# Fifteen 64-byte-row reads behind two input loads in a convolution kernel

## The chip, the cores and the metric

The kernel runs on one core of a Trainium2 chip. The time is device microseconds (us) of one execution. Besides the timed executions one execution was taken by the hardware profiler; the rows that are quoted as profile lines come from that one. Engines are named as in the profile: PE is the matrix engine, PEld its weight load, DVE the vector engine, ACT the scalar engine, POOL the GpSimd engine, SP the SyncE engine, which computes nothing here and issues transfers. A q behind an engine's name is its instruction queue; q0, q1, q10 and so on are queues of transfers, served by 16 DMA engines.

## The reference

The kernel computes a 3x3 convolution with padding 1 of a batch of 16 images, 64 channels in and 128 out, 64 by 64 pixels, in float32 in and out.

```
batch, c_in, h, w, c_out = 16, 64, 64, 64, 128
x_pad = np.pad(x, ((0, 0), (0, 0), (1, 1), (1, 1)), mode='constant')
for b in range(batch):
    for co in range(c_out):
        for ci in range(c_in):
            for kh in range(3):
                for kw in range(3):
                    output[b, co] += weight[co, ci, kh, kw] * x_pad[b, ci, kh:kh+h, kw:kw+w]
```

The input is 16.8 MB, the output 33.6 MB, the weights 0.3 MB.

## The kernel before

Images are taken in pairs: the 64 channels of two images fill the 128 partitions, so there are eight pairs, numbered 0 to 7. Two neighbouring output rows share work: with a row sum `ss` (row 2j plus row 2j+1, line L71) one product with the middle weights serves both. For each pair, four blocks of eight row couples are worked on; in each block PE makes three groups of products (all on line L155): U from `ss`, A and Bt from the 16-bit input `xs`, each for both images into a PSUM tile `acc` (eight of them exist). ACT copies U to `ut` (L169), DVE adds A and `ut` into the even rows of the output tile `ot` (L178) and Bt and `ut` into the odd rows (L181).

Transfers go by three issuing engines. SP issues, in this order, the weights `w_raw` (L42), pair 0 as float32 `x0` (L44), pair 1 as float32 `x1` (L46), and later the stores of the first image of each pair (helper `store`, L111). POOL issues the loads of pairs 2 to 7 straight into 16-bit tiles `xs` (helper `load`, L57): three at the start, three more inside the loop. ACT issues the stores of the second image of each pair, held back until the next block's `ut` copies have been made (also L111). Pairs 0 and 1 are turned to 16 bit on chip by ACT (L96, L175); the row sums of pair 0 are made by DVE, all others by POOL (L71).

`x0`, `x1` and the output tiles share eight 16 KB buffers under the tag `ot`, so stores may run up to four pairs behind the arithmetic. In the last two pairs the stores are cut into halves and quarters.

The order of the work on an engine is that of the program; `keep` fixes it for the copies, sums, loads and held stores. The framework adds all waits. It gives the transfers that SP and ACT issue, in the order of the program, one of eight completion counters in turn; an issue that takes a counter for the second time is preceded by a wait, on the issuing engine, until the counter's previous transfer has landed. Before the change there are 24 such transfers (three loads, 21 stores), so the ninth is the first to wait, and the profile has eight such waits on SP and seven on ACT under L111, of 17 ns each, the first at 52.2 us. POOL's loads have eight counters of their own.

Of the kernel before, what the change touches and what calls it, by code (L numbers as in the profile page):

```python
# [8 lines left out]
F32 = mybir.dt.float32  # L9
# [4 lines left out]
def kernel(  # L14
# [6 lines left out]
    nc = tc.nc  # L21
# [9 lines left out]
    w_flat = weight.rearrange("co ci kh kw -> co (ci kh kw)")  # L31

    const = ctx.enter_context(tc.tile_pool(name="const", bufs=1))
# [10 lines left out]
    nc.sync.dma_start(x0, x_rows[0:128, :, :])  # L44
    x1 = opool.tile([128, H, W], F32, tag="ot", name="x1")
    nc.sync.dma_start(x1, x_rows[128:256, :, :])  # L46
    cuts = [(0, 18), (18, 34), (34, 50), (50, 64)]
    ident = const.tile([128, 128], F16)
    make_identity(nc, ident)
# [168 lines left out]
```

## Time and profile before

| what | value |
|---|---|
| median of three timed executions | 127.23 us (127.17 to 127.58) |
| profiled execution | 128.39 us, of which the span from first to last instruction is 126.6 us |
| PE busy | 106.0 us, from 10.35 us without a longer gap to 115 us |
| DVE, ACT, POOL busy | 83.6, 44.5, 34.6 us |
| HBM read, written | 17.07 MB, 33.55 MB |
| DMA packets | 4330, of them 480 under 512 bytes |
| first load's landing (`x0`) | 9.6 us |
| second load's landing (`x1`) | 19.4 us |
| first store issued by SP, by ACT | 26.23 us, 26.83 us |
| last store issued | 116.48 us |

Busy times are sums over an engine's instructions. The DMA share is the mean busy share of the 16 DMA engines; packets of two queues on one engine may overlap a little, so it can be over 1. A matrix clock of 0.5 at the end of the span belongs to a stretch in which PE has no work.

### The profile page before, as it was taken

Reading aid. Unit: us, or ns where it says so; the run is one execution under the profiler, and the core shown is the slowest. Engines: PE = TensorE matmul, PEld = TensorE weight load, DVE = VectorE, ACT = ScalarE, POOL = GpSimd, SP = SyncE. Lnnn points to the kernel's source line nnn. Section 1 sums busy time; section 2 is a strip of 40 time slices with the busy share of each in tenths; the row PEclk is TensorE's granted clock in tenths of the full one; section 3 lists DMA queues with packets and bytes.
Section 4 is the critical chain, followed back from the end, with each engine's and each line's share of the span. In section 5 each row is a group of like instructions: output and inputs, shape, how many; then the busy total and the mean of one; then the engine's idle time right before and its main releaser. Section 6 shows DMA issues by size and latency. Waiting matters only on the chain.

```text
span 126.6 us, 2412 instructions
## 1 busy us (share of the span) xinstructions
PE 106.0 (84%) x978; PEld 54.3 (43%) x978; DVE 83.6 (66%) x134; ACT 44.5 (35%) x76; POOL 34.6 (27%) x27
## 2 busy tenths in 40 slices
PE   0407999999999999999999999999999999993000
PEld 0303454554555555554555545455554555541000
DVE  0009297787778777877787778777877787777000
ACT  4108937953333333333333333333333333330000
POOL 2700008677007700699770039000000000000000
PEclk9999999999999999999999999999999999999955
DMA  5999999999999999999999999999999999999970
GB/s 148 370 352 331 342 290 210 215 238 318 383 334 331 295 331 357 365 365 344 349 349 362 383 427 419 419 424 450 419 424 419 432 422 414 430 427 418 418 302 22
DMA packets 4330, 44.48 MB, mean 351 GB/s; under 512 B 480, under 2 KB 480, under 8 KB 864
## 3 DMA queue, kind: packets, MB, share of 16 engines
q1 hardware_dynamic: 2016, 21.27, 40.6%
q10 hardware_dynamic: 1440, 16.78, 31.7%
q0 software_dynamic: 864, 6.29, 24.1%
q8 instruction: 7, 0.11, 0.3%
q14 instruction: 3, 0.02, 0.0%
HBM read 17.07 MB, written 33.55 MB: 400 GB/s over the span
## 4 chain that ended last, share of the span: by engine, by line
PE 82%; DMA 7%; DVE 2%; issue 1%; DVEq 0%; SPq 0%
PE acc L155 82%; DMA x<-in_x_dram 7%; DVE ot L178 1%; DVE ss L71 1%; DVE ot L181 0%; DVEq L213 0%; SPq L42 0%; DVEq L178 0%
## 5 line engine op out<-in xcount | busy, mean ns | idle before, releaser
L155 PE MATMUL acc<-xs,Wt 64*128 64x504 f16 (+3 forms) x768 | 88.9, 378 | 0.0
L155 PEld LDWEIGHTS <-Wt 64*128 64x128 f16 x960 | 53.2, 95 | 55.9 <-issue 6.8
L178 DVE TENSOR_TENSOR ot<-acc,ut 128x512 f32<-128x512 f32 x64 | 41.2, 686 | 23.2 <-PE acc L155 18.5
L169 ACT COPY ut<-acc 128x512 f32<-128x512 f32 x64 | 34.4, 589 | 60.8 <-issue 38.5
L181 DVE TENSOR_TENSOR ot<-acc,ut 128x512 f32<-128x512 f32 x64 | 41.1, 685 | 0.0
L155 PE MATMUL acc<-ss,Wt 64*128 64x504 f16 (+1 forms) x192 | 27.0, 384 | 4.6 <-DVE ss L71 4.6
L71 POOL TENSOR_TENSOR ss<-xs 128x1024 f16<-128x1024 f16 x12 | 25.2, 2122 | 10.1 <-DMA xs<-in_x_dram 9.1
L71 DVE TENSOR_TENSOR ss<-x 128x512 f16<-128x512 f32 x4 | 2.6, 686 | 9.6 <-DMA x<-in_x_dram 9.6
L71 POOL TENSOR_TENSOR ss<-x 128x1024 f16<-128x1024 f32 x2 | 4.7, 2356 | 13.4 <-DMA x<-in_x_dram 13.4
L57 POOL DMA_DIRECT2D xs<-in_x_dram x6 | 3.5, 578 | 17.9 <-PE acc L155 16.0
L96 ACT CAST xs<-x 128x1024 f16<-128x1024 f32 (+2 forms) x4 | 4.0, 1053 | 4.0 <-DMA x<-in_x_dram 4.0
L89 PE MATMUL wp<-ident,w 128*64 128x128 f16 x18 | 1.3, 328 | 4.5 <-POOL w L51 4.5
L175 ACT CAST xs<-x 128x1024 f16<-128x1024 f32 x4 | 4.0, 1057 | 0.0
L89 PEld LDWEIGHTS <-w 128*64 128x64 f16 x18 | 1.1, 210 | 4.5 <-POOL w L51 4.5
L91 ACT CAST Wt<-wp 128x384 f16<-128x384 f32 x1 | 0.5, 478 | 3.1 <-PE wp L89 3.1
L91 ACT ACT_TABLE_LOAD x1 | 1.3, 1283 | 0.7 <-PEq L202 0.7
L51 POOL CAST w<-w_raw 128x576 f16<-128x576 f32 x1 | 0.7, 662 | 2.4 <-DMA w_raw<-in_weight_dram 2.4
L98 ACT CAST Wt<-wp 128x384 f16<-128x384 f32 x1 | 0.5, 478 | 0.5 <-DVE Wt L94 0.5
L93 DVE TENSOR_TENSOR Wt<-wp,Wt 128x384 f16<-128x384 f32 x1 | 0.6, 551 | 0.0
L94 DVE TENSOR_TENSOR Wt<-wp,Wt 128x384 f16<-128x384 f32 x1 | 0.5, 548 | 0.0
L99 ACT CAST Wt<-wp 128x384 f16<-128x384 f32 x1 | 0.5, 485 | 0.0
masks.py:199 POOL TENSOR_SCALAR_AFFINE_SELECT ident<-ident 128x128 f16<-128x128 f16 x1 | 0.3, 292 | 0.1
(5 smaller groups left out, 0.6 us busy)
## 6 DMA issues: line engine op xcount, KB each, us to landing
out_dram<-ot SPq DMA_DIRECT2D x6, 2048.0 KB, 19.7
out_dram<-ot ACTq DMA_DIRECT2D x6, 2048.0 KB, 19.3
xs<-in_x_dram POOLq DMA_DIRECT2D x6, 1024.0 KB, 20.5
x<-in_x_dram SPq DMA_DIRECT2D x2, 2048.0 KB, 13.1
out_dram<-ot ACTq DMA_DIRECT2D x4, 1024.0 KB, 11.7
out_dram<-ot SPq DMA_DIRECT2D x3, 1024.0 KB, 12.8
out_dram<-ot SPq DMA_DIRECT2D x2, 512.0 KB, 10.6
w_raw<-in_weight_dram SPq DMA_DIRECT2D x1, 288.0 KB, 3.0
```

The costliest lines, as they stand in the source:

```text
L51: keep(nc.gpsimd.tensor_copy(w16, w_raw))
L57: keep(nc.gpsimd.dma_start(xs[p], x_rows[128 * p : 128 * p + 128, :, :]))
L71: eng.tensor_add(ss[p][:, lo : lo + n, :], v[:, lo : lo + n, 0, :], v[:, lo : lo + n, 1, :])
L89: nc.tensor.matmul(wp[q : q + 64, k * CO : k * CO + CO], w16[:, t::9], ident)
L91: keep(nc.scalar.copy(wrow(G1), wps[1]))
L93: keep(nc.vector.tensor_sub(wrow(G21), wps[2], wrow(G1)))
L96: keep(nc.scalar.copy(xs[0][:, lo:hi, :], x0[:, lo:hi, :]))
L155: nc.tensor.matmul(tiles[b2][:, lo - j0 : hi - j0, c_lo:c_hi], Wt[p0 : p0 + 64, wi, kw, :], rhs, start=i == 0, stop=i == n - 1,)
L169: keep(nc.scalar.copy(ut, U[b2]))
L175: keep(nc.scalar.copy(xs[1][:, lo : lo + 16, :], x1[:, lo : lo + 16, :]))
L178: nc.vector.tensor_add(ots[b2][:, j0 : j0 + RB, 0, :], A[b2], us[b2])
L181: nc.vector.tensor_add(ots[b2][:, j0 : j0 + RB, 1, :], Bt[b2], us[b2])
```

## The change

A spare tile of 16 partitions, 16 rows of 16 float32 each, is made, and behind the load of `x1` fifteen reads are issued from SP. Read n (1 to 15) takes 64 bytes from each of the first n rows of the weights and writes them to the first n partitions of the spare tile. That is 1 + 2 + ... + 15 = 120 rows of 64 bytes, 7,680 bytes together. Nothing reads the spare tile.

```
     nc.sync.dma_start(x0, x_rows[0:128, :, :])
     x1 = opool.tile([128, H, W], F32, tag="ot", name="x1")
     nc.sync.dma_start(x1, x_rows[128:256, :, :])
+    mark = const.tile([16, 16, 16], F32)
+    for n in range(1, 16):
+        nc.sync.dma_start(mark[0:n, n, :], w_flat[0:n, 16 * n : 16 * n + 16])
     cuts = [(0, 18), (18, 34), (34, 50), (50, 64)]
```

The reads take part in the turn of the eight counters: reads 1 to 5 take the five counters not used so far, read 6 that of `w_raw`, read 7 that of `x0`, read 8 that of `x1`, reads 9 to 15 those of reads 1 to 7. The first store (SP) then takes the counter of read 8, the second (ACT) that of read 9. From the ninth store on, each store follows the same earlier store as before.

More of the change, by code (lines that the diff above doesn't have):

```diff
@@ L46 @@
     nc.sync.dma_start(x1, x_rows[128:256, :, :])
+    mark = const.tile([16, 16, 16], F32)
+    for n in range(1, 16):
+        nc.sync.dma_start(mark[0:n, n, :], w_flat[0:n, 16 * n : 16 * n + 16])
     cuts = [(0, 18), (18, 34), (34, 50), (50, 64)]
```

## The prediction

> **What bounds the kernel now.** I began with the chain of waits on the page, which ends on PE:
>
> ```profile
> PE 82%; DMA 7%; DVE 2%; issue 1%; DVEq 0%; SPq 0%
> ```
>
> Read alone, this says that only the landing of x0 at 9.6 us and 104 us of products matter. But the chain stops at the last DVE sum, 116.45 us into a span of 126.6 us; behind it only stores run. So I read the page's slices and then a table of stretches (columns: length, busy time and count of PE, PEld, DVE, ACT, POOL, granted clock, DMA share, GB/s):
>
> ```profile
> DMA  5999999999999999999999999999999999999970
> DMA packets 4330, 44.48 MB, mean 351 GB/s; under 512 B 480, under 2 KB 480, under 8 KB 864
> ```
>
> ```profile
> 4.40:9.60 5.20, 1.31 (x18) 1.23 (x19) 0.00 (x0) 0.48 (x1) 1.70 (x4) 1.00 1.01 381
> 9.60:19.50 9.90, 9.15 (x66) 4.29 (x67) 7.56 (x13) 6.78 (x10) 0.02 (x1) 1.00 1.04 315
> 19.50:26.00 6.50, 6.50 (x64) 3.36 (x62) 5.05 (x9) 5.92 (x8) 4.67 (x2) 1.00 1.01 210
> ...
> 80.00:100.00 20.00, 20.00 (x190) 10.17 (x186) 15.79 (x26) 6.60 (x13) 0.00 (x0) 1.00 1.01 428
> ...
> 117.00:120.00 3.00, 0.00 (x0) 0.00 (x0) 0.00 (x0) 0.00 (x0) 0.00 (x0) 1.00 1.00 414
> 120.00:123.00 3.00, 0.00 (x0) 0.00 (x0) 0.00 (x0) 0.00 (x0) 0.00 (x0) 0.58 0.82 347
> 123.00:126.60 3.60, 0.00 (x0) 0.00 (x0) 0.00 (x0) 0.00 (x0) 0.00 (x0) 0.50 0.07 30
> ```
>
> The share is 1.0 in every stretch from 4.4 to 120 us. The 210 GB/s at 19.5 us is no slack: those are pairs 2 to 4, counted at the 16-bit size written, while twice as much is read. So two bounds lie close together: PE is never idle from 10.35 us on, and the DMA engines have work from 2 to about 122.5 us (0.82 of the 3 us behind 120). The one that ends the kernel is the transfers. At the last issue (116.48 us) about 6 us of work is still queued on every DMA engine, of which the last megabyte itself is 2.5 us at 428 GB/s; arithmetic could end 3.5 us later before the DMA engines ran dry. And the end is that of one DMA engine: the last SP store's sixteen completions, in the trace's landing records, come at 119.4 to 122.6 us for thirteen of them, then 124.2, 124.5 and 125.7.
>
> It follows what to ask of the change: does it give the last DMA engine more work, or does it hold an engine by more than 3.5 us?
>
> **SP's queue.** Start, length, instruction; the loads and the first stores on SP (the third row merges two issues and the time between), then ACT around its first store:
>
> ```profile
> 1.17 0.42 SPq L44 DMA_DIRECT2D x<-in_x_dram  x1
> 1.65 0.42 SPq L46 DMA_DIRECT2D x<-in_x_dram  x1
> 26.23 13.15 SPq L111 DMA_DIRECT2D out_dram<-ot  x2
> ```
>
> ```profile
> 26.16 1.07 ACT L169 COPY ut<-acc 128x512 f32<-128x512 f32 x2 [0.20 <-ACT xs L175]
> 26.83 0.37 ACTq L111 DMA_DIRECT2D out_dram<-ot  x1
> 29.33 1.07 ACT L169 COPY ut<-acc 128x512 f32<-128x512 f32 x2 [2.10 <-DVE ot L181]
> ```
>
> One issue takes 0.42 us and the next follows 0.06 later, so fifteen cost 15 x 0.48 = 7.2 us of SP, which stands idle from 2.07 to 26.23 us. That is cover enough without waits. With the turn of the counters: reads 1 to 5 are out by 4.5 us; read 6 wants w_raw, landed at 3.7, and is out at 5.0; read 7 waits for x0 (9.6) and is out at 10.1; read 8 waits for x1 (19.4) and is out at 19.9; reads 9 to 15 need seven times 0.48, to 23.3 us at the soonest. Behind them on SP stands only the first store, with 2.9 us in hand: cost 0. If that cover went, a store issued later would cost nothing up to the 3.5 us above.
>
> **Waits on landings.** Reads 1 to 7 stand behind x1 in q1 on each DMA engine they use, so x0 and x1 land as before; PE's start, POOL's row sums (19.48) and ACT's casts (20.7) don't move: 0. Even if x1 came later, POOL's sums of pair 1 end at 24.2 us, and PE wants them at 28.4. From 19.4 on the small reads share the engines with pairs 3 and 4 on q0. Between 9.6 and 19.5 us, where x1 and pair 2 ran side by side, the queues had about equal time, row by row; a row of q0 takes 0.63 us (mean of 768 packet records). If a small read waits for one such row, seven are through by 19.4 + 4.4 = 23.8 us, read 8 lands at about 24.5 and read 9 at 25.1: both ahead of the stores that take their counters. If the completion write waits for a row of its own, the seven take 8.8 us; read 8 lands at 29.5 and read 9 at 30.7. Then SP's first store is 3.2 us late and ACT's 3.9 us late; ACT stands still until 31.1 instead of copying at 29.33, 1.8 us late. PE has eight PSUM tiles, four groups, about 3.2 us of lead; nothing is lost there, or at most 1.8 us of the 3.5. The DMA engines are fed meanwhile by pair 4 and by pair 5, issued at 26.02 (2 MB read, 5 us). I take 0, with 0 to 1.8 us of held arithmetic, hidden at the end, as the bounds.
>
> **Work on the DMA engines.** This is what can't hide. The packet records have four sizes: 16,384 bytes in 611 ns, 8,192 (stores) in 309, 4,096 in 159, 2,304 in 93. The last three lie on one line, 9 ns plus 37.5 ns per KB; carried on to 64 bytes it gives 11 ns, an estimate. A completion write of 4 bytes takes 7 to 22 ns, mean 12; every transfer before the change has sixteen (30 transfers, 480 packets under 512 bytes on the page). No row shows a transfer of fewer than 16 rows. Spread evenly, 120 rows are 7.5 on each DMA engine: 7.5 x 11 = 0.08 us, and 15 completions x 12 ns = 0.18 us at most, 0.09 if only engines that carry rows write one. I take the middle of 0.17 and 0.26: 0.2 us. The low end is 0, if the last engine carries none of it; below that, -1.2 us if the last engine's lag over the next (125.7 against 124.5) went away, for which no row speaks. The high end: each row as dear as the nearest row of a load, 93 ns, plus 22 ns, fifteen on one engine: 1.7 us; 0.9 us with 7.5. A first packet of w_raw took up to 714 ns, its latency with nothing ahead of it; later ones of the same ring took 93, and the small reads run beside rows already in flight, so I leave 714 out.
>
> The Trainium skill, in "DMA: Bandwidth & Descriptors", section "Why a DMA increments its semaphore by 16 and not by 1", says that such a transfer uses only as many DMA engines as divide its row counts, the lowest-numbered ones; the first engine would get fifteen rows and the sixteenth none. The same page, "Latency and other measured facts", calls engines 7 and 15 the slow ones as a rule. By the two, the last engine here would get eight rows or none, 8 x 23 ns = 0.2 us or 0, instead of my even spread; no record here names the engine.
>
> The spare tile takes 1 KB in each partition, and no buffer count changes: 0. The end waits for the same counters: 0.
>
> **Sum.** Profiled execution 128.39 (span 126.6 plus 1.8 around it) + 0.2 = 128.6 us. It lies 0.9% above the median of the timed runs, so I carry the difference, not the sum: 127.23 + 0.2 = 127.4 us, no change within 0.3% (0.38 us, about what a measurement of this kernel can tell from none).
>
> **Rivals.** First, slower by dear small packets: place, the last DMA engine between 19.4 and 30 us; price, 0.9 us with 7.5 rows at 115 ns, 128.1 us; 128.9 us with fifteen. It decides as soon as a read costs that engine over 25 ns with fifteen of them, 51 ns with 7.5. For it: the DMA share of 1.0, so nothing is absorbed; against it: the straight line through the packet times and the 12 ns completions. The Trainium skill's "DMA: Bandwidth & Descriptors", "Specifications", speaks for it: under 512 bytes the engine reads, modifies and writes. It gives no price, and no run here shows one for data; by it the time would be this rival's.
>
> Second, slower by a held ACT: read 9 lands so late that ACT's first store holds the copies beyond the 3.5 us in hand. For it: the two-turn reckoning gives 1.8 us of it already; against it: it needs twice that. At 5 us of delay the time is 127.2 + 1.5 + 0.2 = 128.9 us.
>
> Third, faster: the reads or the shifted first stores change which queue an engine serves first, and the last engine's lag of 1.2 us shrinks. 126.0 us if all of it goes, 126.7 with half. For it: the last engine is decided by small things; against it: work is only added.
>
> Fourth, the reads are served in gaps, or not at all: 127.2 us, within the bound.
>
> **How the numbers follow.** Forecast 0.40 and the fourth rival 0.07: same 0.47. Dear packets 0.30, held ACT 0.06, and 0.05 for the forecast's own sum overrun past 0.38 us by a few completions: slower 0.41. Third rival 0.12: faster. The range from 126.8 (half the lag gone and scatter) to 128.6 (dear packets between 7.5 and fifteen rows) leaves about a tenth on each side. The likeliest case's own range is 127.2 to 127.6.
>
> **What would show it.** SP: fifteen more issues of about 0.4 us, the seventh behind 9.6, the eighth behind 19.4 us, the last before 26 us; later than 26.2 says two turns per read. ACT's first store still at 26.8 us and its copy at 29.3. PE starting at 10.35 and ending near 115. DMA: 120 packets more of data, and 120 or 240 completions, each near 10 to 25 ns; over 50 ns, the first rival. The last landing at 125.7 to 126 us. I am wrong if a row shows an engine waiting on a landing of the spare tile for over 3.5 us, or a DMA share below 1 before 120 us.

## The result, and the profile after

The changed kernel took 128.24 us (median of 18, 127.21 to 128.70) against 127.19 us (median of 18, 126.32 to 128.32): ratio 1.0081, 95% interval 1.0059 to 1.0103, so it is slower by 0.6 to 1.0%, or about 1.0 us. The profiled execution took 128.53 us with a span of 126.7 us. That of before had 128.39 and 126.6, and was itself 0.9% above its median; the two spans can therefore not be set against each other, and the readings below are of places inside them.

The page of the kernel after, its DMA busy slices and its packets:

```profile
DMA  5999999999899999999999999999999999999981
DMA packets 4570, 44.48 MB, mean 351 GB/s; under 512 B 720, under 2 KB 720, under 8 KB 1104
```

There are 240 packets more, all under 512 bytes: 120 rows of 64 bytes, and 120 completion writes. And one slice, at 31.7 to 34.8 us, reads 8 where before had a 9 from the second slice to the 38th; that is not yet the finding, since a packet is counted whole in the slice in which it starts.

What SP's queue of the kernel after waited for (total us, times, longest):

```profile
SPq L114 <- DVE ot L184: 83.9, 10, 12.4
SPq L49 <- DMA x<-in_x_dram: 14.9, 2, 9.5
...
SPq L49 <- DMA mark<-in_weight_dram: 5.3, 7, 0.9
SPq L114 <- DMA mark<-in_weight_dram: 1.1, 2, 0.9
```

The two waits for the loads are the ones foreseen (reads 7 and 8). The last two rows are the news: each of reads 9 to 15 waited up to 0.9 us for the read eight places earlier to land, and then the store did too. By the instruction records reads 9 to 15 left at 20.0, 21.2, 22.4, 23.3, 24.3, 25.5 and 26.7 us, about 1.1 us apart. The timeline of SP in the kernel after (start, length), then that of ACT:

```profile
2.11 24.93 SPq L49 DMA_DIRECT2D mark<-in_weight_dram  x15
28.00 24.55 SPq L114 DMA_DIRECT2D out_dram<-ot  x3
```

```profile
26.54 1.07 ACT L172 COPY ut<-acc 128x512 f32<-128x512 f32 x2 [0.20 <-ACT xs L178]
28.36 0.37 ACTq L114 DMA_DIRECT2D out_dram<-ot  x1
29.71 1.07 ACT L172 COPY ut<-acc 128x512 f32<-128x512 f32 x2 [2.10 <-DVE ot L184]
```

The first store left at 28.00 us (before 26.23), ACT's first at 28.36 (26.83). Some 0.4 us of either is not the waits: the arithmetic of this one execution ran that much later (POOL's load of pair 5 at 26.40 against 26.02, ACT's copy at 26.54 against 26.16). ACT's next copy still waited for DVE and not for the store, so the arithmetic was not held. What changed is the feeding of the DMA engines. The same table of stretches as in the prediction (length, busy time of five engines, clock, DMA share, GB/s), before and after:

```profile
26.00:30.00 4.00, 4.00 (x42) 2.05 (x40) 3.32 (x6) 1.75 (x4) 3.96 (x3) 1.00 1.04 256
27.50:29.50 2.00, 2.00 (x22) 0.98 (x18) 2.00 (x4) 0.17 (x1) 2.00 (x2) 1.00 0.94 266
30.00:36.00 6.00, 6.00 (x59) 3.01 (x57) 4.63 (x8) 1.68 (x4) 0.82 (x1) 1.00 1.03 363
```

```profile
26.00:30.00 4.00, 4.00 (x42) 2.11 (x38) 3.40 (x6) 1.70 (x4) 3.58 (x3) 1.00 0.97 167
27.50:29.50 2.00, 2.00 (x22) 1.04 (x20) 1.72 (x3) 0.11 (x1) 2.00 (x2) 1.00 0.85 116
30.00:36.00 6.00, 6.00 (x60) 3.06 (x57) 4.55 (x8) 1.86 (x4) 1.20 (x1) 1.00 1.01 247
```

The share of a stretch counts every packet whole where it starts, and two queues overlap a little, so full stretches of this length read 1.00 to 1.05, and the 0.97 has to be read with the shorter stretch inside it, 0.94 before and 0.85 after. Counting the packets that are open at each moment in the packet records, the sixteen engines together stood idle for 0.37 us a piece between 20 and 44 us, nearly all of it from 27.5 to 29.5; before it was 0.05 us. Pair 4's rows end at 27.6 to 28.0 us on most engines. Pair 5's first rows follow at 27.7 to 28.0 on about ten of them and only from 28.5 on on the others, and they are slow: the rows that start from 27.65 to 29.0 us take 1.05 us on average, where a row in the run of them takes 0.62. The stores that filled this place before (first row at 27.32 us) were not there: SP's first row starts at 32.37 us, 4.4 us behind its issue, ACT's at 32.99. The lower GB/s up to 36 us is no loss by itself: pair 5 went first, and loads count half of what they read, so that 214 GB/s would be a full stretch of loads. The 116 from 27.5 to 29.5 us is little more than half of that. Later on both kernels are full (428 GB/s from 60 to 110 us in either, with a load's row counted at the 16 KB it reads), so that nothing is made up. The end after the change:

```profile
117.00:120.00 3.00, 0.00 (x0) 0.00 (x0) 0.00 (x0) 0.00 (x0) 0.00 (x0) 0.67 1.00 415
120.00:123.00 3.00, 0.00 (x0) 0.00 (x0) 0.00 (x0) 0.00 (x0) 0.00 (x0) 0.50 0.94 393
123.00:126.70 3.70, 0.00 (x0) 0.00 (x0) 0.00 (x0) 0.00 (x0) 0.00 (x0) 0.50 0.18 73
```

### The profile page after: what moved, and what is told of

Same layout as the page of the kernel before. It is cut to its first block, busy times and chain, and to the rows that moved or that the text cites. A ratio compares the mean times of both kernels' runs of the same rounds, so it can differ in the third digit from the quotient of the medians.

```text
span 126.7 us, 2433 instructions
## 1 busy us (share of the span) xinstructions
PE 106.6 (84%) x978; PEld 55.3 (44%) x978; DVE 83.7 (66%) x134; ACT 44.5 (35%) x76; POOL 34.7 (27%) x27
## 4 chain that ended last, share of the span: by engine, by line
PE 82%; DMA 6%; DVE 2%; issue 1%; DVEq 0%; SPq 0%
PE acc L158 82%; DMA x<-in_x_dram 6%; DVE ot L181 1%; DVE ss L74 1%; DVEq L216 0%; DVE ot L184 0%; SPq L42 0%; DVEq L181 0%
## 5 line engine op out<-in xcount | busy, mean ns | idle before, releaser
L158 PEld LDWEIGHTS <-Wt 64*128 64x128 f16 x960 | 54.2, 96 | 55.4 <-issue 7.1
```

The source lines that it names most:

```text
L158: nc.tensor.matmul(tiles[b2][:, lo - j0 : hi - j0, c_lo:c_hi], Wt[p0 : p0 + 64, wi, kw, :], rhs, start=i == 0, stop=i == n - 1,)
```

## The experiments

Theory 1: the reads hold the first stores by the turn of the counters; the stores' rows miss the moment at which pair 4's run out, and the DMA engines stand. Theory 2, the first rival of the prediction: the small packets themselves are dear on the last DMA engine. Ratios are to the kernel before, runs on the same chip; the idle time is that of the sixteen engines between 20 and 44 us, worked out from the packet records in the same way for each profile. It counts an engine with an open packet as busy, however slowly that packet moves. Each profile is one execution, in which the arithmetic stands up to 1 us earlier or later than in the next (pair 5's load is issued at 25.4 to 27.0 us).

**Twelve reads instead of fifteen.** The edit takes three reads away, and with them three steps of the turn:

```
-    for n in range(1, 16):
+    for n in range(4, 16):
```

> The reads of 4 to 15 rows alone: 12 reads, 114 of the 120 rows. With three counters fewer taken, the first store (SP) follows the counter of the fifth read, the second (ACT) that of the sixth, which in the changed kernel's trace landed at 24.8 and 26.0 us, so the stores leave at about 26.3 and 26.9 us. Theory 1 (the stores held by the counters leave the DMA engines short of work around 28 to 30 us; 0.37 us there against 0.05 before): the loss goes, ratio to before 1.000 to 1.003. Theory 2 (the rows and completions themselves cost the last DMA engine about 1 us): 12 of 15 parts of it stay, ratio 1.006 to 1.007.

Ratio 1.0051 (1.0019 to 1.0083), 127.78 us. Neither number: the stores left on time, yet well over half of the loss (0.51 of 0.81%) stayed. SP's timeline and the stretch:

```profile
19.19 3.73 SPq L49 DMA_DIRECT2D mark<-in_weight_dram  x5
26.19 13.17 SPq L114 DMA_DIRECT2D out_dram<-ot  x2
```

```profile
26.00:30.00 4.00, 4.00 (x42) 2.06 (x38) 3.28 (x6) 1.78 (x4) 3.98 (x3) 1.00 0.94 181
```

The gap is there (0.94; idle 0.26 us): the store's first row started at 28.62 us, 2.4 us behind its issue, against 1.1 us before. By the wait alone this store was free. The reads that still stood ahead of it in the same ring, whose last rows were served at 27.76 us, are the likeliest hold that is left; no run shows it by itself. So theory 1 as first put, with the wait on SP as the only hold, was too narrow.

**Stores held without reads, by small copies.** Pair 0's two stores were taken out of their place and put behind a 64-byte copy, on SP and on ACT, that reads pair 1's first sum:

```
+            if p == 1 and blk == 0:
+                src = ots[0][0:1, j0, 0, 0:16]
+                keep(nc.sync.dma_start(mark[0:1, 0, :], src))
+                keep(store(nc.sync, *late.pop()))
+                keep(nc.scalar.dma_start(mark[0:1, 1, :], src))
+                keep(store(nc.scalar, *held.pop(0)))
```

> No reads; pair 0's two stores each stand behind a copy of 64 bytes that waits for the first even-row sum of pair 1, so that they leave at about 28.4 and 28.5 us instead of 26.2 and 26.8. Theory 1: the DMA engines run short from 28.3 to about 29.5 us as in the changed kernel, ratio to before 1.003 to 1.008. Theory 2: two rows are nothing, ratio 1.000 within 0.2%.

Ratio 1.0165 (1.0129 to 1.0200), 129.12 us, above the range given. Both stores left at 28.02 us, and their rows started at 33.6 and 34.3: even the small copies, issued at 27.4, reached the DMA engines only at 32.3, when pair 5's rows were nearly through. Theory 2 has nothing to say to a loss of 2 us with no reads in it. The profiled execution, the fastest of the six, shows only 0.17 us of idle, so this run does not tie the size of the loss to the gap, and its small copies leave a doubt, which the hold without them below takes up.

**Many more rows, no wait.**

```
+    mark = const.tile([128, 5, 16], F32)
+    for n in range(5):
+        nc.sync.dma_start(mark[:, n, :], w_flat[:, 16 * n : 16 * n + 16])
```

> Five reads of 64 bytes from all 128 rows: 640 rows, 40 on each DMA engine, and 80 completions; the counters are new ones, so no store is held. Theory 1: only the time of the packets, at the 24 ns of a row in the changed kernel's records: 40 x 24 ns = 0.96 us, with completions 1.0 us, ratio 1.008; if they are hidden, 1.000. Theory 2 needs about 70 ns for a row (1 us for fifteen of them on one engine), so 40 cost 2.7 us, ratio 1.021.

Ratio 1.0018 (0.9997 to 1.0040), 127.37 us. The page of this kernel has the 720 packets more than before (640 rows, 80 completions):

```profile
DMA packets 5050, 44.52 MB, mean 355 GB/s; under 512 B 1200, under 2 KB 1200, under 8 KB 1584
```

```profile
26.00:30.00 4.00, 4.00 (x42) 2.05 (x40) 3.14 (x6) 1.90 (x4) 3.98 (x3) 1.00 1.09 280
```

Forty rows on each DMA engine cost 0.2 us, at most 0.5 by the interval: 6 ns a row, at most 13. The change has at most fifteen on one. Theory 2 falls. No gap in the stretch; the stores left at 26.05 and 26.66 us.

**Stores held further, to block 2.** The same edit as the run with small copies, with `blk == 2`.

> As the run with stores held to 28 us, but held for the first even-row sum of block 2 of pair 1, at about 34.6 us. Theory 1: the load of pair 5 alone feeds the DMA engines from about 29 to 33.5 us, then they stand nearly still until the stores' first rows at about 36; with the first gap 2 to 3 us are lost and not made up, ratio 1.015 to 1.025. Theory 2: ratio 1.000 within 0.2%.

Ratio 1.0323 (1.0285 to 1.0361), 131.20 us, above the range given. The stretches of this kernel:

```profile
26.00:30.00 4.00, 4.00 (x42) 2.06 (x38) 2.83 (x5) 1.82 (x4) 3.98 (x3) 1.00 0.91 174
30.00:36.00 6.00, 6.00 (x60) 2.99 (x56) 5.03 (x8) 1.27 (x3) 0.34 (x1) 1.00 0.61 115
```

Pair 5 alone fed the engines to about 33 us, then they stood: 2.69 us of idle, and 4.1 us lost. This is the largest gap and the largest loss, with the arithmetic ending as early as before (last issue at 115.99 us against 116.48).

**A hold by DVE, which did not hold.** One element of each of pair 0's output tiles is written onto itself behind pair 1's first sums, so that the stores have to wait for it:

```
                 nc.vector.tensor_add(ots[b2][:, j0 : j0 + RB, 0, :], A[b2], us[b2])
+                if p == 1 and blk == 0:
+                    one = (late if b2 == 0 else held)[0][2][0:1, 0, 0, 0:1]
+                    nc.vector.tensor_copy(one, one)
```

> No reads and no small transfers: DVE writes one element of each of pair 0's output tiles onto itself behind the first even-row sums of pair 1, so the two stores can leave only at 28.1 to 28.9 us instead of 26.2 and 26.8. Theory A (a late first store is enough: pair 5's rows go first on every DMA engine, there is a gap behind pair 4 near 28 us, and the stores' rows start near 33 us): ratio to before 1.006 to 1.016. Theory B (small transfers stuck in the store queue did it in the reads' kernel and in the run held to 28): 1.000 to 1.003, the stores' rows starting at about 29.5 us.

Ratio 1.0019 (0.9988 to 1.0050). The planner moved the two copies ahead of the sums, so the stores were not held: they left at 26.47 and 27.07 us, 0.24 us late, as did the load of pair 5 (26.26), and the idle time was 0.06 us. It decides nothing between the theories; what it shows is that a shift of 0.24 us of both doesn't open the gap.

**The same hold, with the order fixed.** Both the sum and the copy are kept in program order:

```
+                    keep(even)
+                    keep(nc.vector.tensor_copy(one, one))
```

> The pure hold again, with the copies now tied behind pair 1's first even-row sums (in the run before this one the planner had moved them ahead, and the stores left at 26.5 us): no reads, no small transfers, SP's first store leaves at about 28.2 us, ACT's at about 29. Theory A (a late first store is enough): the DMA share drops below 0.95 between 27.5 and 29.5 us, pair 5's rows go first, the stores' rows start at 32 to 34 us, ratio to before 1.006 to 1.016. Theory B (the reads' own standing in the ring is needed): the stores' rows start about 1.5 us behind their issue, ratio 1.000 to 1.004.

Ratio 1.0125 (1.0088 to 1.0162), 128.55 us. SP's store and the stretch:

```profile
28.77 11.21 SPq L112 DMA_DIRECT2D out_dram<-ot  x2
```

```profile
26.00:30.00 4.00, 4.00 (x42) 2.27 (x38) 3.40 (x9) 1.70 (x4) 3.21 (x3) 1.00 0.84 145
```

Not one packet is added to the kernel before (its page has the same 4330), and the whole picture of the change is there: the stores leave 2.5 us late, the gap opens (0.72 us of idle), SP's rows start at 32.98 us. Lateness of the first two stores is enough for the loss. The size of the gap in this one profile is not theirs alone: pair 5's load, too, was issued 0.75 us later here (26.77 us) than in the kernel before. That a late load is not needed is shown by the hold to block 2, where it was issued early (25.54 us) and the loss was the largest.

**The reads with the gap filled.** Six input buffers instead of five, with pair 5's load issued at the start; first with the fifteen reads, then without them.

```
-    xpool = ctx.enter_context(tc.tile_pool(name="xpool", bufs=5))
+    xpool = ctx.enter_context(tc.tile_pool(name="xpool", bufs=6))
-    for p in range(2, 5):
+    for p in range(2, 6):
-        if p > 0 and p + 4 < NP:
+        if p > 1 and p + 4 < NP:
```

> The fifteen reads as in the change, but six input buffers instead of five, with pair 5's load issued at the start behind pair 4's, so that nothing can run dry near 28 us. Theory A with the gap as the cause: the stores still leave at about 28 us and their rows start behind pair 5's near 33 us, but the time is that of the kernel before with six buffers within 0.3%. If the order of the rows is the cause and not the gap, it stays 0.5 to 1% above that kernel.

> The kernel before with six input buffers and pair 5's load issued at the start: the base for the run of the reads with six buffers. All DMA engines stay busy; with the gap as the cause, ratio to before 0.998 to 1.003. If an early pair 5, whose rows go ahead of the first stores, costs by itself, 1.005 or more.

Ratios 1.0018 (0.9999 to 1.0038) with the reads, 0.9992 (0.9971 to 1.0013) without. SP's timeline and the stretch with the reads:

```profile
19.33 7.94 SPq L49 DMA_DIRECT2D mark<-in_weight_dram  x8
28.24 11.54 SPq L114 DMA_DIRECT2D out_dram<-ot  x2
```

```profile
26.00:30.00 4.00, 4.00 (x42) 2.06 (x38) 3.40 (x6) 1.70 (x4) 3.98 (x4) 1.00 1.04 212
27.50:29.50 2.00, 2.00 (x22) 1.03 (x20) 1.73 (x3) 0.10 (x1) 1.98 (x3) 1.00 1.06 214
```

The first store is as late as in the change (28.24 us), its rows start as late (32.88), the reads are all there; only the gap is gone (idle 0.01 us), because pair 5's rows stand behind pair 4's without a break. From 27.5 to 29.5 us it moves 214 GB/s, all loads, where the change moved 116; at 214 the difference is 0.9 us of feeding. The ratio falls from 1.0081 to 1.0018, which is 0.8 us. So the order in which pair 5 and the stores are served is not what costs most, nor are the rows: it is the gap. What is left over the base with six buffers is small but there: the means of the two kernels' twelve runs differ by 0.30 us, with a standard error of 0.08. The expectation had allowed it (within 0.3%), and where it comes from was not tested.

**Fifteen reads of one row each.**

```
-        nc.sync.dma_start(mark[0:n, n, :], w_flat[0:n, 16 * n : 16 * n + 16])
+        nc.sync.dma_start(mark[0:1, n, :], w_flat[0:1, 16 * n : 16 * n + 16])
```

> Fifteen reads of one row of 64 bytes each, so 15 rows instead of 120, with the same turn of counters. Theory A: the reads pass one DMA engine one by one as before, so SP's first store still leaves near 28 us, ratio to before 1.005 to 1.010. If the number of rows matters: an eighth of the loss, 1.000 to 1.002.

Ratio 1.0067 (1.0033 to 1.0101), 128.36 us. An eighth of the rows, and the loss is there:

```profile
27.18 13.18 SPq L114 DMA_DIRECT2D out_dram<-ot  x2
```

```profile
26.00:30.00 4.00, 4.00 (x41) 2.04 (x38) 3.40 (x6) 1.98 (x3) 3.01 (x3) 1.00 0.87 154
```

The loss did not shrink with the rows, so it is not their number that counts. The profile is a poorer witness than the time: in this execution the whole arithmetic was 0.95 us late (pair 5's load at 26.97 us), and SP's store at 27.18 us had waited for DVE and not for a read; only ACT's, at 28.02, was held, by 0.2 us. SP's first row then started at 29.79 us, 2.6 us behind its issue, with the reads ahead of it in the ring (last rows at 27.68 us), as in the run with twelve. The 0.56 us of idle can't be put down to the late rows alone, since the load was late too.

**Eight reads.**

```
-    for n in range(1, 16):
+    for n in range(8, 16):
```

> The reads of 8 to 15 rows alone (8 reads, 92 rows): SP's first store follows the counter of the first read, landed near 20 us, so both stores leave on time, at 26.2 and 26.8 us; the last reads still stand ahead of the store's rows in the ring. If only the counters' waits hurt: ratio to before 1.000 to 1.002, share near 1.0 throughout. If the reads standing in the ring delay the store's rows past the end of pair 4's (27.9 us): a gap near 28 us as in the run with twelve reads, ratio 1.002 to 1.006.

Ratio 1.0025 (0.9993 to 1.0057), 127.41 us. Stretch and SP's timeline:

```profile
26.00:30.00 4.00, 4.00 (x42) 2.13 (x38) 2.66 (x6) 1.63 (x4) 3.98 (x3) 1.00 1.02 324
```

```profile
2.11 17.56 SPq L49 DMA_DIRECT2D mark<-in_weight_dram  x8
25.55 0.38 SPq L114 DMA_DIRECT2D out_dram<-ot  x1
```

The store's rows started at 27.47 us and there was no idle time; the arithmetic of this execution was early (pair 5's load at 25.51 us). The trace answers for the first of the two cases of the expectation; the ratio's interval takes in both. That the point at which the reads reach past the end of pair 4's rows lies between eight reads (no gap) and twelve (0.26 us) is what these two profiles suggest, not more.

## Why the prediction was right or wrong

The measured median, 128.24 us, lies in the range (126.8 to 128.6), but the likeliest case, 127.4 us and no change, was not what came; slower had 0.41. That the range held is luck: its upper end was set by dear packets, which the run with 640 rows rules out. The sign that the prediction named for being wrong, a DMA share below 1 before 120 us, came: 0.85 from 27.5 to 29.5 us, though in a stretch this short the kernel before reads 0.94 itself.

- **The bound.** Right, and it carried everything: the DMA engines are nearly full from 2 to about 120 us, and every run that let them stand for over 0.1 us was slower, whatever PE did. In the run held to block 2 the arithmetic ended earlier than before and the kernel 4.1 us later.
- **SP's issues.** Fifteen of 0.24 to 0.36 us rather than 0.42. The reads that had a free counter were out by 3.7 us. No harm either way.
- **The waits on landings.** Both ways were worked out, one or two rows of q0 for each small read; the trace lies near the second (reads 9 to 15 about 1.1 us apart, two rows of 0.63 us being 1.26). SP's first store was 1.8 us late where the two-turn reckoning had 3.2, ACT's 1.5 where it had 3.9, and 0.4 us of either was the arithmetic of that execution. That nothing of it reaches the arithmetic was right: ACT's copy at 29.71 us waited for DVE.
- **"The DMA engines are fed meanwhile by pair 4 and by pair 5".** This is the step that failed. Pair 5 was issued at 26.02 us before and 26.40 after. After the change its first rows began 1.3 us behind that at the earliest, from 28.5 us on on several engines, and took 1.05 us each instead of 0.62, while pair 4's ended at 27.6 to 28.0; the rows of the stores were what had filled this place. I had counted a transfer as feeding at full rate from its issue on. And the same lateness was set to 0 by the 3.5 us in hand at the end, which is the slack of the arithmetic, not of a DMA engine that is full to the end: a moment in which it stands is lost.
- **The work of the small packets.** 0.2 us was the estimate; the run with 640 rows puts forty rows at 0.2 us, so the change's 7.5 to 15 rows on an engine are below 0.2. The records have 8 to 24 ns for a row of 64 bytes (mean 19) and 120 completions, not 240: a read of n rows completed n times. That is what the Trainium skill states in "DMA: Bandwidth & Descriptors", section "Why a DMA increments its semaphore by 16 and not by 1"; the trace agrees.
- **The first rival**, dear small packets, gave the right size (128.1 us) for the wrong reason. Its rule, in "Specifications" of the same page of the Trainium skill (reads and modifies below 512 bytes), shows no price here: 6 ns a row, at most 13.
- **The second rival**, a held ACT, was the nearest in mechanism: a store held by a read's counter. It looked for the price at ACT's copies; it was at the DMA engines.

The size of the loss is only partly accounted for. The idle time is a lower bound, since it does not see slow rows. The bytes do: 428 GB/s is full (a load's row counted at the 16 KB it reads), and what a profile moved less than that between 20 and 44 us can be put in us.

| kernel | idle, us | moved too little, us | lost by the ratio, us |
|---|---|---|---|
| before | 0.05 | 0.9 | |
| fifteen reads (the change) | 0.37 | 2.1 | 1.0 |
| hold by DVE | 0.72 | 2.4 | 1.6 |
| hold to block 2 | 2.69 | 3.8 | 4.1 |
| fifteen reads of one row | 0.56 | 1.5 | 0.9 |
| twelve reads | 0.26 | 1.2 | 0.6 |
| hold by small copies | 0.17 | 1.3 | 2.1 |
| fifteen reads, six buffers | 0.01 | 1.0 | 0.2 |
| six buffers, no reads | 0.03 | 0.8 | -0.1 |
| hold that did not hold | 0.06 | 0.9 | 0.2 |
| 640 rows | 0.00 | 0.5 | 0.2 |
| eight reads | 0.00 | 0.2 | 0.3 |

Each of the six kernels that lose over 0.5 us moved too little by 1.2 us or more, and none of the others by more than 1.0. For the change and the hold by DVE the excess over the kernel before, 1.2 and 1.4 us, is about the loss. For the hold to block 2 it is 2.9 of 4.1, and for the hold by small copies 0.4 of 2.1, so there the size stays open. The first two columns are single executions of kernels that scatter by about 1%; that of the kernel before took 1.2 us more than its median with hardly any idle, so that a microsecond can also come from elsewhere.

## What to carry to other kernels

Where the DMA engines set the time and are full to the end, ask of a change first whether at any moment the rings run empty; a late store costs nothing on its own engine and can still cost a good part of its lateness there (1.0 us of 1.8 here, 4.1 of 8.5 in the hold to block 2). A small transfer counts by the ring and the counter that it takes, not by its bytes: behind fifteen of them a 2 MB store left 1.8 us late and began 5 us late. And a gap of that kind was closed here by queueing the next load early, behind the one that is running out: 1.0081 became 1.0018.

## What the runs showed of the hardware

- A ring that gets work while another ring's rows are in service did not get its turn at once. After the change SP's first store was issued at 28.00 us and its first row started at 32.37, after most of pair 5's eight rows an engine; in the hold by DVE 28.77 and 32.98; in the hold to block 2 SP's store, issued at 34.75, started at 39.91, behind six rows of ACT's, issued at 34.74. In the kernel before the same step took 1.1 us (26.23 to 27.32). Once both had rows in service, they took turns: in the kernel before fourteen of the open packets are SP's at 30.75 us and fourteen are ACT's at 31.25. Why the first turn came so late, no record shows.
- Small reads queued in one ring, beside another ring full of 16 KB rows, landed about 0.9 to 1.2 us apart in the change, mostly nearly two rows of 0.63 us. This is read from the issues of reads 9 to 15, each of which waits for an earlier one; with one row each (20.13 to 25.52 us for five steps) the mean is the same 1.1 us.
- The first rows of a load that reached engines that had run empty took longer: 1.05 us on average in the change (rows started from 27.65 to 29.0 us), 0.62 with six buffers, where none had run empty.
- The issue of a read on SP took 268 ns with seven rows and 323 with fifteen, against 332 to 425 for the 128-row transfers. The first six reads, issued back to back, scatter from 235 to 355.
